# RWKV-7 recurrence on one core: odd units in the opposite partition halves, one PSUM bank per unit, and y as r·P times the state plus one product with [u; v]

## The chip, the cores and the metric

One core of one Trainium2 chip. The metric is the device time of one execution in microseconds. Three runs of the kernel before gave 2138.86, 2139.52 and 2139.69 us; the median is 2139.52. An effect of about 0.2%, some 4.3 us, can be told from no change.

## The reference

One inference step of a decoder trunk with two layers, for a prompt group (16 meta tokens and 256 prompt tokens, 272 in all) and a sample group of 8 sequences with one token each. Layer A is RWKV-7 time mixing with 64 heads of 64 channels, layer B sliding-window attention. All numbers are float32. What the change touches is layer A's recurrence over the 272 prompt tokens:

```python
def rwkv7_step(S, inp):
    r, d, k, v, kk, b = inp
    sa = jnp.einsum('bhij,bhj->bhi', S, kk)
    S = S * d[:, :, None, :] - sa[..., None] * b[:, :, None, :] + v[..., None] * k[:, :, None, :]
    return S, jnp.einsum('bhij,bhj->bhi', S, r)
...
S_fin, y = lax.scan(rwkv7_step, S0.astype(f32),
                    (tm(r_h), tm(d_h), tm(k_h), tm(v_h), tm(kk), tm(b_h)))
```

The result y is then normalised per head, gated and projected; the final state S is an output.

## The kernel before

**Chunks.** The scan runs in five chunks per head: four of 64 tokens and one of 16. P is the running product of the decays inside a chunk. With v the values of a chunk, and u the corrections that the term sa·b makes, a chunk is
- W = (kk·P)ᵀ times the state + a masked score matrix times v,
- u = TT·W, where TT solves the triangular system of the chunk,
- state = (state + BKᵀ[u; v]) times the decay,
- y = (r·P)ᵀ times the state at the start + masked scores times u and v.

**Units, groups and halves.** A unit u is two channel planes of 128 (index j), each with two heads in its two partition halves (q = 0, 1); H(q) is half q. Sixteen units; a group o is two units, an even and an odd one, 8 heads. For each head, X[c] holds 128 rows: H(q) first the state and later u, the other half v. So one product over 128 rows takes the state's and v's part together.

**What is prepared.** `prep_e` (L945) writes KB (keys and b over P) and E, two tiles of 128x2x544: for each chunk 64 columns of kk·P, then 64 of r·P. E1 is a copy of E0's upper half (L968). `scores` (L971) multiplies KB with E into two PSUM banks of [128, 512], one for each q. From each bank ACT copies the triangular parts into F and ND (L1005, L1006) for the solve, and DVE writes the masked scores: for v into the other half of E (L1007), for u into a tile RB (L1009). Even units, and some of the steps of the odd ones, use the two buffers of the pool `pe`; odd units alternate them with the single-bank pools `pc` and `py`. `substitute` (L1040) and `solve` (L1076) make TT for a group.

**The chain** (L1144). For each chunk, with three blocks on PE and pauses between them:
- S1: W into a bank of `pc` (L1173, 8 products), and y's part of state and v into a bank of `py` (L1177, 8 products). ACT copies W to SBUF (L1180, L1183).
- S2: TT times W, again into the bank of W (L1188, 8 products of 64 rows, or of 16 in the last chunk). ACT copies u over the state in X (L1190).
- S3: the state's growth (L1191, 8 products over 128 rows) and y's part of u (L1193, 8 products over 64 rows), both into the bank of `py`. DVE adds the growth to the state and applies the decay (L1201, L1202, L1204), ACT and DVE copy the state to the next X (L1207), ACT copies y to Y (L1209).

In both units a head with q = 0 takes W, u and y in partitions 0 to 63 and one with q = 1 in 64 to 127. In the first chunk the state is zero, and POOL clears that half of X[0] (L1140).

After the chain, `group_norm` (L1229) normalises Y on DVE and turns it back: for j = 0 to 3 three transposes into one bank, of `py` for even j and `pc` for odd j (L1246), which DVE reads (L1247).

**What sets the order.** PE's order is written out: `drive` (L599) puts out pieces of the projection products, each 6 products of L208 to L210 with 280 columns, and between two pieces lets the streams (`preps`, `main` with chain, scores and solve, `group_norm`, `decodes`) put out their next block when they have paused for the number of pieces that they yielded. The chain yields 5 pieces ahead of S1, 2 ahead of S2, 3 ahead of S3; group_norm 36 ahead of its first transposes and 3 ahead of each further one. Each engine works through its own queue in order. The other engines' orders come from the framework's scheduler, which also places the semaphores: for PSUM it keeps readers and writers of one tile apart, readers on different engines too.

Of the kernel before, what the change touches and what calls it, by code (L numbers as in the profile page):

```python
# [22 lines left out]
E = 4096  # L23
# [86 lines left out]
class Kernel:  # L110
# [10 lines left out]
    def run(self):  # L121
        nc, tc = self.nc, self.tc
        with contextlib.ExitStack() as st:
            pool = lambda n, bufs=1, **k: st.enter_context(tc.tile_pool(name=n, bufs=bufs, **k))
            self.cp = pool("const")
            self.wp = pool("wts", 5)
            self.pm = pool("pm", 3, space=PSUM)
            self.pp = pool("pp", 1, space=PSUM)
            self.pe = pool("pe", 2, space=PSUM)
            self.pc = pool("pc", 1, space=PSUM)  # L130
            self.py = pool("py", 1, space=PSUM)
# [11 lines left out]
            self.phase_a()  # L143
            self.close("mix")
# [11 lines left out]
            self.close("gB", "g1", "st1", "wx1", "g0", "at", "res")  # L156
# [788 lines left out]
    def prep_e(self, u):  # L945

        nc, rp = self.nc, self.rp
        V, A, G = nc.vector, nc.scalar, nc.gpsimd
        tt = V.tensor_tensor
        MU = ALU.mult  # L950
        kT, rT, kk, a, cl = (self.U[u][n] for n in ('kT', 'rT', 'kk', 'a', 'cl'))
        Pp = self.Pp
        ch = lambda x: x[:, :, :256].rearrange("p q (c t) -> p q c t", t=64)
        pch = Pp[:, :, :260].rearrange("p q (c t) -> p q c t", t=65)
        KB = self.KB
        tt(KB[:, :, 0:4, 64:128], ch(kT), ch(cl), op=MU)
# [6 lines left out]
        ech = lambda e: e[:, :, :512].rearrange("p q (c t) -> p q c t", t=128)  # L963
        tt(ech(E[0])[:, :, :, 0:64], ch(kk), pch[:, :, :, 0:64], op=MU)
        tt(ech(E[0])[:, :, :, 64:128], ch(rT), pch[:, :, :, 1:65], op=MU)
        tt(E[0][:, :, 512:528], kk[:, :, 256:272], Pp[:, :, 260:276], op=MU)
        tt(E[0][:, :, 528:544], rT[:, :, 256:272], Pp[:, :, 261:277], op=MU)
        A.copy(E[1][64:128], E[0][64:128])  # L968
        self.U[u]['E'] = E

    def scores(self, u):  # L971
# [5 lines left out]
        banks = lambda nm: [self.bank(p, f"ps_{nm[0]}{q}{nm[1]}") for q, p in  # L977
                            enumerate((self.pc, self.py) if next(turn) else (self.pe, self.pe))]
# [6 lines left out]
        RB = rp.tile([128, 2, L], F32, tag="RB", bufs=3, name=f"RB{u}")  # L985
        BK = rp.tile([128, 2, 5, 128], F32, tag="BK", bufs=3, name=f"BK{u}")
        self.U[u].update(RB=RB, BK=BK)
        inst = lambda a, r, cs: a[r, i0:i0 + 8].rearrange("p (a c) t -> p a c t", c=4)[:, :, cs]
        bc = lambda m, *s: m.unsqueeze(1).unsqueeze(1).to_broadcast(s)
        for c0 in (0, 2):  # L990
# [4 lines left out]
            with self.pe_order():  # L995
                for j in range(2):
                    for c in range(2):
                        for q in (1, 0):
                            o = 128 * (c0 + c)
                            nc.tensor.matmul(ps[q][:, j, c], KB[H(q), j, c0 + c, 64 * q:64 * q + 128],  # L1000
                                             E[q][H(q), j, o:o + 128], start=True, stop=True)
            for q in range(2):
                pv, kr, br = ps[q], H(1 - q), H(q)
                r1, r2 = slice(64 * q, 64 * q + 32), slice(64 * q + 32, 64 * q + 64)
                A.copy(inst(self.F, r1, cs), pv[r1, :, :, 0:64])  # L1005
                A.copy(inst(self.ND, r2, cs), pv[r2, :, :, 32:64])  # L1006
                tt(E[q][kr, :, 128 * c0:128 * c0 + 256].rearrange("p a (c t) -> p a c t", c=2), pv[kr],  # L1007
                   bc(self.cst(C_MASK, 128, kr), 64, 2, 2, 128), op=MU)
                tt(RB[br, :, 64 * c0:64 * c0 + 128].rearrange("p a (c t) -> p a c t", c=2), pv[br, :, :, 64:128],  # L1009
                   bc(self.cst(C_MASK + 64, 64, br), 64, 2, 2, 64), op=MU)  # L1010
        yield next(gap)
        ps = [b[:, :64].rearrange("p (a h t) -> p a h t", a=2, h=2) for b in banks(("sc", f"4_{u}"))]
        with self.pe_order():
            for j in range(2):
                for q in (1, 0):
                    nc.tensor.matmul(ps[q][:, j], KB[H(q), j, 4, 64 * q:64 * q + 128], E[q][H(q), j, 512:544],
                                     start=True, stop=True)
        for q in range(2):
            pv, kr, br = ps[q], H(1 - q), H(q)
            r1 = slice(64 * q, 64 * q + 32)  # L1020
            m = self.cst(C_MASK, 128, kr).rearrange("p (h t) -> p h t", h=2)[:, :, 0:16]
            A.copy(self.ND[r1, 16 + i0 // 4:18 + i0 // 4, 0:16], pv[r1, :, 0])
            tt(E[q][kr, :, 512:544].rearrange("p a (h t) -> p a h t", h=2), pv[kr],
               m.unsqueeze(1).to_broadcast((64, 2, 2, 16)), op=MU)
            tt(RB[br, :, 256:272], pv[br, :, 1],
               self.cst(C_MASK + 64, 16, br).unsqueeze(1).to_broadcast((64, 2, 16)), op=MU)
# [99 lines left out]
    def load_x(self, o):  # L1126
# [12 lines left out]
        for q in range(2):  # L1139
            G.memset(X[0][H(q), q], 0.0)  # L1140
# [3 lines left out]
    def chain(self, o):  # L1144
# [11 lines left out]
        heads = [(j, q) for j in range(4) for q in range(2)]  # L1156
        E = lambda j, q: us[j // 2]['E'][q][:, j % 2]
        S = FS
        decay = lambda c: PC[:, :, c:c + 1].to_broadcast((128, 4, 64))
        for c in range(5):  # L1160
# [4 lines left out]
            R = lambda q: slice(64 * q, 64 * q + n)  # L1165

            ry = lambda q: H(q) if c < 4 else slice(64 * q + 32, 64 * q + 48)
            yield (5 if c else 3), (None if c or not o else self.after(2, ('g', o - 1)))
            wu = self.bank(self.pc, f"ps_wu{o}_{c}").rearrange("p (k a i) -> p k a i", k=2, a=4)
            sy = self.bank(self.py, f"ps_sy{o}_{c}").rearrange("p (k a i) -> p k a i", k=2, a=4)  # L1170
            with self.pe_order():
                for j, q in heads:
                    mm(wu[R(q), 0, j], E(j, q)[:, 128 * c:128 * c + n], x[:, q, j], start=True, stop=True)  # L1173

                for j, q in heads:
                    out, k = (H(q), 128 * c + 64) if c < 4 else (slice(64 * q, 64 * q + 48), 496)
                    mm(sy[out, 1, j], E(j, q)[:, k:k + out.stop - out.start], x[:, q, j], start=j == 0, stop=False)  # L1177
            W = rp.tile([128, 4, 64], F32, tag="W", name=f"W{o}_{c}")
            if c < 4:
                A.copy(W, wu[:, 0])  # L1180
            else:
                for q in range(2):
                    A.copy(W[R(q)], wu[R(q), 0])  # L1183
            yield 2
            with self.pe_order():
                for j, q in heads:
                    lhs = TT[H(q), 4 * j + c] if c < 4 else TT[R(q), 16 + j, 0:16]
                    mm(wu[R(q), 1, j], lhs, W[R(q), j], start=True, stop=True)  # L1188
            for q in range(2):
                A.copy(x[R(q), q], wu[R(q), 1])  # L1190
            grow = lambda j, q, stop: mm(sy[H(q), 0, j], us[j // 2]['BK'][:, j % 2, c, H(q)], x[:, q, j],  # L1191
                                         start=False, stop=stop)
            of_u = lambda j, q, stop: mm(sy[ry(q), 1, j], us[j // 2]['RB'][R(q), j % 2, 64 * c:64 * c + n],  # L1193
                                         x[R(q), q, j], start=False, stop=stop)
            yield 3
            with self.pe_order():
                for i, f in enumerate((grow, of_u) if c < 4 else (of_u, grow)):
                    for j, q in heads:
                        f(j, q, i == 1 and j == 3)
            if c:  # L1200
                V.tensor_tensor(S, S, sy[:, 0], op=AD)  # L1201
                V.tensor_tensor(S, S, decay(c), op=MU)  # L1202
            else:
                V.tensor_tensor(S, sy[:, 0], decay(c), op=MU)  # L1204
# [3 lines left out]
            for q in range(2):  # L1208
                A.copy(self.Y[64 * (c % 2):64 * (c % 2) + n, c // 2, :, q], sy[ry(q), 1])  # L1209
# [3 lines left out]
        dma(self.O['wkv'][o], FS)  # L1213

# [14 lines left out]
    def group_norm(self, o):  # L1229
# [10 lines left out]
        for j in range(4):  # L1240
# [3 lines left out]
            ps = self.bank((self.py, self.pc)[j % 2], f"ps_yt{o}_{j}")  # L1244
# [699 lines left out]
```

## Time and profile before

| what | value |
|---|---|
| median of three runs | 2139.52 us (2138.86 to 2139.69) |
| span of the profiled execution | 2135.9 us; what lies around it is 3.6 us against that median |
| PE / DVE / ACT / POOL busy, share of the span | 98% / 80% / 59% / 6% |
| TensorE clock granted | 0.97 to 1.00 in every stretch |
| recurrence (first S1 to last S3) | 276.6 to 1252 us of the span |

The profile is of one execution. Its timeline gives, per row, the start in us, the length, engine, line, operation, output and inputs, shape and count; where an engine was idle ahead of it, the idle time and what ended it follow in brackets. Its view by groups gives busy us (the union of the instructions), the mean length of one in ns, and the idle time of the engine just before them. A float32 product leaves two records on PE. Names are those of the program, with buffer numbers left out.

### The profile page before, as it was taken

To read this page: it belongs to the slowest core of one execution; us is meant where nothing else is said; L and a number is where in the kernel's file an instruction comes from. 1 tells how busy PE (TensorE), PEld (TensorE's weight loads), DVE (VectorE), ACT (ScalarE), POOL (GpSimd) and SP (SyncE) were. 2 spreads that over 40 slices of the span, in tenths; PEclk is the share of its full clock that TensorE was granted. 3 is DMA by queue.
4 is the path that set the end of the run, shared out by engine and by line. 5 is a ranking of instruction groups with operands and counts; after the bars stand their busy time and mean duration, and the time that the engine had idled before them with its cause. 6 is when DMAs were issued, how large, how long until landed. Compare 5 with 4: busy or idle time off the path is not lost.

```text
span 2135.9 us, 56097 instructions
## 1 busy us (share of the span) xinstructions
PE 2093.4 (98%) x21548; PEld 1989.4 (93%) x21548; DVE 1706.2 (80%) x4080; ACT 1261.2 (59%) x2757; POOL 136.5 (6%) x196
## 2 busy tenths in 40 slices
PE   9999999999999999999999999999999999999997
PEld 7999998899899989999989999999999999999997
DVE  7867767787687777888978787987888888878885
ACT  3457756576765667766675445565565555644443
POOL 0011100001010010100200000100000000000000
PEclk9999999999999999999999999999999999999999
DMA  7998667658756766777656777757445454567774
GB/s 257 316 318 248 192 203 229 210 178 278 220 169 193 252 228 184 219 226 207 203 152 219 219 230 247 244 184 228 144 147 167 140 157 134 179 205 248 224 224 134
DMA packets 276357, 446.30 MB, mean 209 GB/s; under 512 B 54056, under 2 KB 97768, under 8 KB 275696
## 3 DMA queue, kind: packets, MB, share of 16 engines
q1 hardware_dynamic: 275656, 441.66, 66.7%
q8 instruction: 169, 2.77, 0.5%
q10 hardware_dynamic: 432, 1.05, 0.1%
q14 instruction: 100, 0.82, 0.1%
HBM read 381.69 MB, written 65.03 MB: 209 GB/s over the span
## 4 chain that ended last, share of the span: by engine, by line
PE 89%; DVE 4%; DMA 3%; ACT 2%; issue 1%; SPq 1%; POOL 0%; DVEq 0%; POOLq 0%; ACTq 0%
PE ps_z L208 6%; PE ps_z L209 6%; PE ps_z L210 5%; PE ps_v L208 3%; PE ps_r L208 3%; PE ps_ob L208 3%; PE ps_ob L210 3%; PE ps_ob L209 3%; PE ps_k L208 3%; PE ps_v L209 3%; PE ps_v L210 3%; PE ps_r L209 3%; PE ps_r L210 3%; PE ps_q L208 3%; PE ps_q L210 3%; PE ps_q L209 3%
## 5 line engine op out<-in xcount | busy, mean ns | idle before, releaser
L208 PE MATMUL ps_z<-mhlm,whi_z 128*128 128x280 f32 x512 | 158.7, 310 | 0.4 <-ACT st L779 0.4
L208 PE MATMUL ps_q<-bmh,whi_qb 128*128 128x264 f32 x512 | 149.9, 293 | 0.1
L209 PE MATMUL ps_z<-mhlm,whi_z 128*128 128x280 f32 x512 | 149.9, 293 | 0.0
L210 PE MATMUL ps_z<-mhlm,wlo_z 128*128 128x280 f32 x512 | 149.5, 292 | 0.0
L208 PE MATMUL ps_z<-bmh,whi_zb 128*128 128x264 f32 x512 | 147.4, 288 | 0.0
L210 PE MATMUL ps_q<-bmh,wlo_qb 128*128 128x264 f32 x512 | 145.7, 284 | 0.6 <-DVE wlo_qb L187 0.6
L209 PE MATMUL ps_q<-bml,whi_qb 128*128 128x264 f32 x512 | 145.6, 284 | 0.0
L209 PE MATMUL ps_z<-bml,whi_zb 128*128 128x264 f32 x512 | 145.5, 284 | 0.0
L210 PE MATMUL ps_z<-bmh,wlo_zb 128*128 128x264 f32 x512 | 145.4, 284 | 0.0
L208 PE MATMUL ps_ob<-ghi,whi_ob 128*128 128x264 f32 x512 | 145.3, 285 | 0.0
L209 PE MATMUL ps_ob<-glo,whi_ob 128*128 128x264 f32 x512 | 144.6, 283 | 0.0
L210 PE MATMUL ps_ob<-ghi,wlo_ob 128*128 128x264 f32 x512 | 144.6, 284 | 0.0
L185 ACT CAST whi_ob<-raw_ob 128x512 fp32r<-128x512 f32 x128 | 79.1, 621 | 96.9 <-PE ps_ob L209 76.5
L185 ACT CAST whi_oa<-raw_oa 128x512 fp32r<-128x512 f32 x128 | 79.4, 621 | 90.7 <-PE ps_oa L209 32.4
L187 DVE TENSOR_TENSOR wlo_r<-raw_r,whi_r 128x512 fp32r<-128x512 f32 x128 | 87.7, 689 | 49.2 <-ACT whi_r L185 46.3
L208 PE MATMUL ps_v<-mhlm,whi_v 128*128 128x280 f32 x384 | 121.5, 316 | 1.2 <-ACT st L779 1.2
L208 PE MATMUL ps_k<-mhlm,whi_k 128*128 128x280 f32 x384 | 119.2, 310 | 0.9 <-ACT st L779 0.9
L187 DVE TENSOR_TENSOR wlo_v<-raw_v,whi_v 128x512 fp32r<-128x512 f32 x128 | 87.2, 686 | 39.5 <-ACT whi_v L185 38.8
L185 ACT CAST whi_v<-raw_v 128x512 fp32r<-128x512 f32 x128 | 79.0, 618 | 65.3 <-PE ps_v L209 39.5
L185 ACT CAST whi_zb<-raw_zb 128x512 fp32r<-128x512 f32 x128 | 78.2, 619 | 62.6 <-PE ps_z L209 40.0
L187 DVE TENSOR_TENSOR wlo_oa<-raw_oa,whi_oa 128x512 fp32r<-128x512 f32 x128 | 87.5, 689 | 32.8 <-ACT whi_oa L185 31.2
L209 PE MATMUL ps_v<-mhlm,whi_v 128*128 128x280 f32 x384 | 112.7, 293 | 0.0
(474 smaller groups left out, 7681.5 us busy)
## 6 DMA issues: line engine op xcount, KB each, us to landing
raw_k<-a_w_rkvz SPq DMA_DIRECT2D x128, 256.0 KB
raw_v<-a_w_rkvz SPq DMA_DIRECT2D x128, 256.0 KB
raw_r<-a_w_rkvz SPq DMA_DIRECT2D x128, 256.0 KB
raw_z<-a_w_rkvz SPq DMA_DIRECT2D x128, 256.0 KB
raw_oa<-a_w_out SPq DMA_DIRECT2D x128, 256.0 KB
raw_qb<-b_w_qz SPq DMA_DIRECT2D x128, 256.0 KB
raw_zb<-b_w_qz SPq DMA_DIRECT2D x128, 256.0 KB
raw_ob<-b_w_o SPq DMA_DIRECT2D x128, 256.0 KB
```

The lines of the kernel that those rows point to most:

```text
L185: self.nc.scalar.copy(hi, src)
L187: return self.nc.vector.tensor_tensor(lo, src, hi.bitcast(F32), op=ALU.subtract)
L208: mm(ps, wh, xh, start=start, stop=False)
L209: mm(ps, wh, xl, start=False, stop=False)
L210: return mm(ps, wl, xh, start=False, stop=stop)
```

## The change

The mirrored layout. In odd units the products of a head with half q now land in half 1-q of PSUM where W, TT and y are concerned, while X, KB, E and the state stay as they were. The rows of F and ND that the odd units write are exchanged to match (`r ^ 64 * odd`), and Y is read back through an access pattern of its own (`turned_y`).

The banks. During phase A the pools `pc` and `py` are closed, and one pool `pcy` with a single tile of two banks takes their place: bank f belongs to unit f of the group and holds all four regions of a chunk (W, u, growth, y). The odd units' scores, their transposes and group_norm's transposes take the same tile, bank by bank.

The terms of y. E is now [128, 5, 2, 272]: E[:,0] and E[:,1] are kk·P and the masked scores of v for the two halves, E[:,2] is r·P, and E[:,3] and E[:,4] hold the masked scores of y for all 128 rows, u's and v's. RB is gone. y is (r·P)ᵀ times the state (64 rows, in S2 behind TT, not in the first chunk) plus one product over 128 rows with [u; v] (in S3). In the first chunk W is a product over the 64 rows of v alone, so X[0] is not cleared. In the last chunk POOL clears W, and TT and the product run over all 64 rows.

```diff
@@ run
+            self.close("py", "pc")
+            self.pcy = self.open("pcy", 1, space=PSUM)
             self.phase_a()
+            self.close("pcy")
+            self.single_banks()
...
+    def two_banks(self, name):
+
+        return self.pcy.tile([128, 2, 512], F32, tag="b", name=name)
@@ prep_e
-        E = [rp.tile([128, 2, 544], F32, tag=f"E{q}", bufs=3, name=f"E{q}_{u}") for q in range(2)]
...
-        A.copy(E[1][64:128], E[0][64:128])
+        E = rp.tile([128, 5, 2, L], F32, tag="E", bufs=3, name=f"E_{u}")
+        tt(ch(E[:, 0]), ch(kk), pch[:, :, :, 0:64], op=MU)
+        tt(ch(E[:, 2]), ch(rT), pch[:, :, :, 1:65], op=MU)
...
+        A.copy(E[64:128, 1], E[64:128, 0])
@@ scores
+        rows = lambda q, j, a, b: E[H(q), q:3:2 - q, j, a:b]
...
-                A.copy(inst(self.F, r1, cs), pv[r1, :, :, 0:64])
-                A.copy(inst(self.ND, r2, cs), pv[r2, :, :, 32:64])
-                tt(E[q][kr, :, 128 * c0:128 * c0 + 256].rearrange("p a (c t) -> p a c t", c=2), pv[kr],
-                   bc(self.cst(C_MASK, 128, kr), 64, 2, 2, 128), op=MU)
-                tt(RB[br, :, 64 * c0:64 * c0 + 128].rearrange("p a (c t) -> p a c t", c=2), pv[br, :, :, 64:128],
-                   bc(self.cst(C_MASK + 64, 64, br), 64, 2, 2, 64), op=MU)
+                for r, a, t0 in ((64 * q, self.F, 0), (64 * q + 32, self.ND, 32)):
+                    A.copy(inst(a, slice(r ^ 64 * odd, (r ^ 64 * odd) + 32), cs), pv[r:r + 32, :, :, t0:64])
+                tt(out(q, kr), pv[kr, :, :, 0:64], bc(self.cst(C_MASK, 64, kr), 64, 2, 2, 64), op=MU)
+                tt(out(3 + q, slice(0, 128)), pv[:, :, :, 64:128], bc(self.cst(C_MASK + 64, 64), 128, 2, 2, 64), op=MU)
@@ load_x
-        for q in range(2):
-            G.memset(X[0][H(q), q], 0.0)
@@ chain
-        heads = [(j, q) for j in range(4) for q in range(2)]
+        heads = [(f, k, q) for k in range(2) for f in range(2) for q in range(2)]
...
-            wu = self.bank(self.pc, f"ps_wu{o}_{c}").rearrange("p (k a i) -> p k a i", k=2, a=4)
-            sy = self.bank(self.py, f"ps_sy{o}_{c}").rearrange("p (k a i) -> p k a i", k=2, a=4)
+            two = self.two_banks(f"ps_ch{o}_{c}")
+            ps = two.rearrange("p f (r k i) -> p f r k i", r=4, k=2)
...
-                for j, q in heads:
-                    mm(wu[R(q), 0, j], E(j, q)[:, 128 * c:128 * c + n], x[:, q, j], start=True, stop=True)
-
-                for j, q in heads:
-                    out, k = (H(q), 128 * c + 64) if c < 4 else (slice(64 * q, 64 * q + 48), 496)
-                    mm(sy[out, 1, j], E(j, q)[:, k:k + out.stop - out.start], x[:, q, j], start=j == 0, stop=False)
+                for f, k, q in heads:
+                    v = H(1 - q) if c == 0 else slice(0, 128)
+                    mm(ps[R(q ^ f), f, 0, k], E(f, q, v, k, 64 * c, 64 * c + n), x[v, q, 2 * f + k],
+                       start=True, stop=True)
...
+                G.memset(W, 0.0)
                 for q in range(2):
-                    A.copy(W[R(q)], wu[R(q), 0])
+                    A.copy(W2[R(q)], part(0, R(q)))
...
+                for f, k, q in heads:
+                    h, j = q ^ f, 2 * f + k
+                    mm(ps[H(q), f, 1, k], TT[H(h), 4 * j + c if c < 4 else 16 + j], W[H(h), j], start=True, stop=True)
+
+                for f, k, q in heads if c else ():
+                    mm(ps[ry(q ^ f), f, 3, k], E(f, 2, H(q), k, *ty), x[H(q), q, 2 * f + k], start=k == 0, stop=k == 1)
...
+                for f, k, q in heads:
+                    add(ps[H(q), f, 2, k], us[f]['BK'][:, k, c, H(q)], x[:, q, 2 * f + k])
+
+                for f, k, q in heads:
+                    add(ps[ry(q ^ f), f, 3, k], E(f, 3 + q, slice(0, 128), k, *ty), x[:, q, 2 * f + k])
@@ group_norm
-            ps = self.bank((self.py, self.pc)[j % 2], f"ps_yt{o}_{j}")
+            if j % 2 == 0:
+                two = self.two_banks(f"ps_yt{o}_{j}")
+            ps = two[:, j % 2]
```

How the instructions stand now, at three places. First PE, the blocks S2 and S3 of chunk 2 in group 3 (units 6 and 7; the pieces of projection products between them are left out). Before:

```order
L1188 MATMUL ps_wu3_2_10843<-W3_2_10864,TT3_9598 64x64 [waits Activation_49]
L1188 MATMUL ps_wu3_2_10843<-W3_2_10864,TT3_9598 64x64 x7
...
L1191 MATMUL ps_sy3_2_10844<-X0_3_9320,BK6_8280 64x64 [waits Activation_49] x2
L1191 MATMUL ps_sy3_2_10844<-X0_3_9320,BK6_8280 64x64 x2
L1191 MATMUL ps_sy3_2_10844<-X0_3_9320,BK7_9299 64x64 x4
L1193 MATMUL ps_sy3_2_10844<-X0_3_9320,RB6_8279 64x64 x4
L1193 MATMUL ps_sy3_2_10844<-X0_3_9320,RB7_9298 64x64 x4
```

And of the change:

```order
L1201 MATMUL ps_ch3_2_10762<-W3_2_10774,TT3_9532 64x64 [waits Activation_49]
L1201 MATMUL ps_ch3_2_10762<-W3_2_10774,TT3_9532 64x64 x7
L1204 MATMUL ps_ch3_2_10762<-X0_3_9257,E_6_8080 64x64 x2
L1204 MATMUL ps_ch3_2_10762<-X0_3_9257,E_7_9230 64x64 x2
L1204 MATMUL ps_ch3_2_10762<-X0_3_9257,E_6_8080 64x64 x2
L1204 MATMUL ps_ch3_2_10762<-X0_3_9257,E_7_9230 64x64 x2
...
L1210 MATMUL ps_ch3_2_10762<-X0_3_9257,BK7_9236 64x64 x2
L1213 MATMUL ps_ch3_2_10762<-X0_3_9257,E_6_8080 64x64 x2
L1213 MATMUL ps_ch3_2_10762<-X0_3_9257,E_7_9230 64x64 x2
L1213 MATMUL ps_ch3_2_10762<-X0_3_9257,E_6_8080 64x64 x2
L1213 MATMUL ps_ch3_2_10762<-X0_3_9257,E_7_9230 64x64 x2
```

The units alternate after every two products. Eight products of y with the state have moved from S1 to the end of S2, and the second half of S3 reads E in place of RB. Second, PE at group_norm's transposes in group 0, without the products between them. Before:

```order
L1246 MATMUL ps_yt0_0_5388<-consts_78,Y_1737 128x128 x3
...
L1246 MATMUL ps_yt0_1_5423<-consts_78,Y_1737 128x128 x3
...
L1246 MATMUL ps_yt0_2_5480<-consts_78,Y_1737 128x128 [waits DVE_49]
L1246 MATMUL ps_yt0_2_5480<-consts_78,Y_1737 128x128 x2
...
L1246 MATMUL ps_yt0_3_5595<-consts_78,Y_1737 128x128 [waits DVE_49]
L1246 MATMUL ps_yt0_3_5595<-consts_78,Y_1737 128x128 x2
```

And of the change:

```order
L1271 MATMUL ps_yt0_0_5365<-consts_78,Y_1742 128x128 x3
...
L1271 MATMUL ps_yt0_0_5365<-consts_78,Y_1742 128x128 [waits DVE_49]
L1271 MATMUL ps_yt0_0_5365<-consts_78,Y_1742 128x128 x2
...
L1271 MATMUL ps_yt0_2_5456<-consts_78,Y_1742 128x128 [waits DVE_49]
L1271 MATMUL ps_yt0_2_5456<-consts_78,Y_1742 128x128 x2
...
L1271 MATMUL ps_yt0_2_5456<-consts_78,Y_1742 128x128 [waits DVE_49]
L1271 MATMUL ps_yt0_2_5456<-consts_78,Y_1742 128x128 x2
```

Before, j = 2 waits for DVE's read of j = 0 and j = 3 for that of j = 1; now j = 1, 2 and 3 each wait for the read of the one just before. Third, ACT at the scores of unit 11 (chunks 2 and 3, copies into F). Before:

```order
L1005 COPY F_1733<-ps_sc12_11_13869 32x2x128 [waits PE_49]
L1006 COPY F_1733<-ps_sc12_11_13869 32x2x2x32
L1005 COPY F_1733<-ps_sc02_11_13868 32x2x128 [waits PE_49]
L1006 COPY F_1733<-ps_sc02_11_13868 32x2x2x32
L185 CAST whi_z_0_14_14026<-raw_z_0_14_14024 128x512 [waits DMAHW7_49,DVE_49,PE_49]
```

And of the change:

```order
L1019 COPY F_1738<-ps_sc2_11_13759 32x2x128 [waits PE_49]
L1019 COPY F_1738<-ps_sc2_11_13759 32x2x2x32
L195 CAST whi_z_0_14_13916<-raw_z_0_14_13914 128x512 [waits DMAHW4_49,DVE_49,PE_49]
...
L1019 COPY F_1738<-ps_sc2_11_13759 32x2x128 [waits DVE_49]
L1019 COPY F_1738<-ps_sc2_11_13759 32x2x2x32
```

The second bank's copies have moved behind DVE's masks of the first bank, and behind the cast that stood after them.

More of the change, by code (lines that the diff above doesn't have):

```diff
@@ L155, in run, with single_banks @@
             self.wx = None
[L156 removed]
+            self.close("gB", "g1", "st1", "wx1", "g0", "at", "res", "py", "pc")
+    def single_banks(self):
+        self.pc, self.py = (self.open(n, 1, space=PSUM) for n in ("pc", "py"))
+    def two_banks(self, name):
+        return self.pcy.tile([128, 2, 512], F32, tag="b", name=name)
     def open(self, name, bufs=1, **k):
@@ L976, in scores, with banks @@
         turn = iter((0, odd, 0, odd, 0))
-        banks = lambda nm: [self.bank(p, f"ps_{nm[0]}{q}{nm[1]}") for q, p in
-                            enumerate((self.pc, self.py) if next(turn) else (self.pe, self.pe))]
+        def banks(nm):
+            if next(turn):
+                two = self.two_banks(f"ps_{nm[0]}{nm[1]}")
+                return [two[:, q] for q in range(2)]
+            return [self.bank(self.pe, f"ps_{nm[0]}{q}{nm[1]}") for q in range(2)]
         V, A, G = nc.vector, nc.scalar, nc.gpsimd
@@ L1207, in chain @@
                     (V.tensor_copy if q else A.copy)(X[c + 1][H(q), q], S[H(q)])
-            for q in range(2):
-                A.copy(self.Y[64 * (c % 2):64 * (c % 2) + n, c // 2, :, q], sy[ry(q), 1])
+            for h in range(2):
+                A.copy(self.turned_y(c, h, n), part(3, slice(ry(h).stop - n, ry(h).stop)).rearrange("p f (k i) -> p f k i", k=2))
             if c % 2 or c == 4:
@@ L1213, in chain, with turned_y @@
         dma(self.O['wkv'][o], FS)
+    def turned_y(self, c, h, n):
+        y = self.Y[64 * (c % 2):64 * (c % 2) + n, c // 2]
+        (step, rows), free = y.ap[0], y.ap[1:]
+        assert [list(a) for a in free] == [[128, 4], [64, 2], [1, 64]], free
+        return type(y)(y.tensor, y.offset + 64 * h, [[step, rows], [320 - 128 * h, 2], [128, 2], [1, 64]])
     def variance(self, o, c):
```

68 lines of the change are left out of this document (29 added, 39 removed).

## The prediction

> **What bounds the kernel now.** I read the stretch of the recurrence first: busy time of each engine between 276 and 1256 us (the columns after the length are PE, PE's weight loads, DVE, ACT, POOL, each with its instructions, then the granted clock, the DMA share and GB/s).
>
> ```profile
> core 0 of [0], span 2135.9 us
> core 0: us, PE busy (x) PEld busy (x) DVE busy (x) ACT busy (x) POOL busy (x), PEclk, DMA share, GB/s
> 276.00:1256.00 980.00, 961.27 (x12209) 895.92 (x12208) 778.33 (x1722) 637.49 (x1404) 78.58 (x115) 0.99 0.68 208
> ```
>
> PE is busy 98% of these 980 us at a clock of 0.99, DVE 79%, ACT 65%, and the DMA engines are at 0.68. So the stretch is bound by PE, and what shortens PE's own list shortens the kernel one for one, as long as nobody new makes PE wait. Who makes it wait today, in us, times and the longest:
>
> ```profile
> PE ps_so L1089 <- DVE TN L1068: 5.0, 2, 2.8
> PE ps_yt L1246 <- DVE vT L1247: 4.0, 1, 4.0
> ```
>
> These two are the longest waits of the whole execution. They are small, but both are places that the change touches.
>
> **The price of a block on PE.** The recurrence is cut into small blocks that stand between the large projection products (L208 to L210). A busy PE says little about such a block, because instructions overlap; so I take the timeline of PE and measure from the last projection product ahead of a block to the second one behind it, less two regular steps. First product of a chunk (S1, ps_wu and ps_sy):
>
> ```profile
> 289.51 0.29 PE L209 MATMUL ps_k<-mhlm,whi_k 128*128 128x280 f32 x1
> 289.64 0.29 PE L210 MATMUL ps_k<-mhlm,wlo_k 128*128 128x280 f32 x1
> 289.86 0.69 PE L1173 MATMUL ps_wu<-X,E 128*64 128x64 f32 x16
> 290.38 0.64 PE L1177 MATMUL ps_sy<-X,E 128*64 128x64 f32 x16
> 290.94 0.40 PE L208 MATMUL ps_k<-mhlm,whi_k 128*128 128x280 f32 x1
> 291.18 0.29 PE L209 MATMUL ps_k<-mhlm,whi_k 128*128 128x280 f32 x1
> ```
>
> A regular step is 289.64 - 289.51 = 0.13. S1 costs 291.18 - 289.64 - 0.26 = 1.28 us for 32 records (each f32 product leaves two). The product with TT (S2) and the last block of a chunk (S3):
>
> ```profile
> 293.76 0.29 PE L210 MATMUL ps_k<-mhlm,wlo_k 128*128 128x280 f32 x1
> 293.98 0.68 PE L1188 MATMUL ps_wu<-W,TT 64*64 64x64 f32 x16
> 294.59 0.40 PE L208 MATMUL ps_k<-mhlm,whi_k 128*128 128x280 f32 x1
> 294.82 0.29 PE L209 MATMUL ps_k<-mhlm,whi_k 128*128 128x280 f32 x1
> ```
>
> ```profile
> 297.68 0.29 PE L210 MATMUL ps_k<-mhlm,wlo_k 128*128 128x280 f32 x1
> 297.90 0.69 PE L1191 MATMUL ps_sy<-X,BK 128*64 128x64 f32 x16
> 298.51 0.68 PE L1193 MATMUL ps_sy<-X,RB 64*64 64x64 f32 x16
> 299.13 0.40 PE L208 MATMUL ps_k<-mhlm,whi_k 128*128 128x280 f32 x1
> 299.36 0.29 PE L209 MATMUL ps_k<-mhlm,whi_k 128*128 128x280 f32 x1
> ```
>
> S2 costs 0.80 us for 16 records. S1 and S2 together give a fixed price of 0.32 and 0.030 per record. S3 costs 1.42 with 32 records, 0.14 more than S1: in its middle PE goes from tiles of 128 rows to tiles of 64 (0.61 from L1191 to L1193, where L1173 to L1177 took 0.52).
>
> **How many tiles run at once** is the open number. Today the products alternate between two tiles, and 0.030 per record means that two overlap (alone, one would take 0.059). The changed S2 names four tiles of 64x64 in turn: rows and columns (0,0), (64,64), (64,0), (0,64). The nearest rows are those of the block solve, where L1089 uses four 32x32 tiles and L1107 two (here: busy us, mean ns | idle before):
>
> ```profile
> L1173 PE MATMUL ps_wu<-X,E 128*64 128x64 f32 x512 | 22.3, 228 | 2.3 <-DVE X L1207 1.4 <-ACT X L1207 0.9
> L1188 PE MATMUL ps_wu<-W,TT 64*64 64x64 f32 x512 | 21.8, 224 | 0.0
> L1177 PE MATMUL ps_sy<-X,E 128*64 128x64 f32 x512 | 20.5, 222 | 0.0
> L1089 PE MATMUL ps_so<-TN,Noff 32*32 32x16 f32 x1024 | 10.3, 184 | 5.0 <-DVE TN L1068 5.0
> L1107 PE MATMUL ps_so<-TN,F 32*32 32x32 f32 x512 | 9.6, 192 | 0.9 <-DVE TN L1102 0.9
> ```
>
> Four tiles made 1024 records in 10.3 us, two made 512 in 9.6: double the rate. Those four share neither rows nor columns; the new four do. But L1173's two tiles share all 128 rows and L1188's share none, and 512 records take 22.3 and 21.8 us, so shared rows cost nothing visible. The bounds are 0.059 (one at a time) and 0.010 (L1089's rate); I take 0.015, four at a time, being the rate of two, doubled as in the solve.
>
> The Trainium skill speaks against it: "TensorE: Matmul & The Clock Gate", Part 3 (packing small matmuls), says that a weight load runs beside a matmul only where the row groups differ. By that rule the pairs with equal rows would not overlap and S2 would keep two at a time, which is the first rival below; L1173 against L1188 disagrees with the rule for tiles of 128 rows, and no row shows it for four tiles of 64.
>
> **The sum on PE** (8 groups of 5 chunks: 32 chunks after the first, 8 first ones):
> - S1 in 32 chunks: 16 records instead of 32, 1.28 to 0.80: -15.4.
> - First chunks, without a state: S1 becomes 16 records on four tiles, 0.32 + 16 x 0.015 = 0.56 (-0.72); S2 with TT alone 0.80 to 0.56 (-0.24): 8 x 0.96 = -7.7.
> - S2 in 32 chunks: 32 records, 0.32 + 32 x 0.015 = 0.80: 0.
> - S3 in 40 chunks: no change of tile, 1.42 to 1.28: -5.6.
>
> Together -28.7.
>
> **What DVE, ACT and POOL gain** is credited with nothing, because PE does not wait for it:
>
> ```profile
> L1007 DVE TENSOR_TENSOR E<-ps_sc,consts 64x512 f32<-64x512 f32 x64 | 43.6, 682 | 10.0 <-ACT F L1006 9.7
> L1009 DVE TENSOR_TENSOR RB<-ps_sc,consts 64x256 f32<-64x256 f32 x64 | 27.0, 422 | 0.9
> L968 ACT COPY E<-E 64x1088 f32<-64x1088 f32 x16 | 17.6, 1100 | 2.0 <-DVE E L967 1.4
> ```
>
> The masks become two of 256 elements: 64 x (682 - 422) = 16.6 us less on DVE. The copy of E halves: some 8 us less on ACT. The memset of W (POOL) may start when S2 of chunk 3 is done, and is needed some eight pieces of the products later.
>
> **The waits it adds.** All readers and writers of the new two-bank tile are ordered as of one tile. In group_norm the transposes of j=1, 2, 3 now each wait for DVE's read of the one before (today j waits for j-2). What stands behind them is everything on PE. First and last of the 8 groups, PE and DVE:
>
> ```profile
> 377.21 0.49 PE L1246 MATMUL ps_yt<-consts,Y 128*128 128x128 f32 x3
> 383.99 0.90 PE L1246 MATMUL ps_yt<-consts,Y 128*128 128x128 f32 x3 [3.97 <-DVE vT L1247]
> ```
>
> ```profile
> 383.46 0.47 DVE L1247 SCALAR_TENSOR_TENSOR vT<-ps_yt,par,vT 128x272 f32<-128x272 f32 x1
> ```
>
> ```profile
> 1272.88 0.49 PE L1246 MATMUL ps_yt<-consts,Y 128*128 128x128 f32 x3
> 1275.54 0.49 PE L1246 MATMUL ps_yt<-consts,Y 128*128 128x128 f32 x3
> ```
>
> ```profile
> 1273.30 0.50 DVE L1247 SCALAR_TENSOR_TENSOR vT<-ps_yt,par,vT 128x272 f32<-128x272 f32 x1
> ...
> 1278.16 0.50 DVE L1247 SCALAR_TENSOR_TENSOR vT<-ps_yt,par,vT 128x272 f32<-128x272 f32 x1
> ```
>
> Group 0: the read of j=0 ends at 383.93, j=1 stood at 377.21, so PE waits 6.7 where it waited 4.0: +2.7. Group 7: j=2 waits 0.9, and j=3, then at 1276.4, for 1278.66: +3.1 in all. The same reading gives 0, 0, 0, 1.3, 0.3 and 1.9 for groups 1 to 6. Together +9.3; 0 if DVE gets there earlier, and I keep 9.
>
> In odd scores ACT's copies of the second bank now wait for DVE's masks of the first; substitute and then the solve (the 5.0 above) stand behind them. The worst of the two solves that wait today:
>
> ```profile
> 887.53 0.26 ACT L1006 COPY F<-ps_sc 32x128 f32<-32x128 f32 x1
> ```
>
> ```profile
> 890.28 0.43 DVE L1009 TENSOR_TENSOR RB<-ps_sc,consts 64x256 f32<-64x256 f32 x1
> ```
>
> The copies would end 890.71 + 0.62 - 887.79 = 3.5 later. The bounds are 0 and 7 for both; I take 1, since the masks in between are four times 0.26 shorter.
>
> U's copies now wait for the y product behind TT in the same block, 0.24 to 0.48 later. The tightest place:
>
> ```profile
> 333.28 0.75 ACT L1190 COPY X<-ps_wu 16x256 f32<-16x256 f32 x2
> ```
>
> ```profile
> 334.11 0.62 PE L1193 MATMUL ps_sy<-X,RB 16*16 16x64 f32 x16
> ```
>
> 0.08 is left there, at one of 40 chunks (1.1 us of ACT just ahead of it is the copy of E that halves): nothing. The next S1 waits for Y's copies at its start instead of 0.52 into it; L1177's idle time of 0.0 says that they are long done: nothing.
>
> **Sum:** -28.7 + 9.3 + 1 = -18.4, from a span of 2135.9 to 2117.5. The median of the three runs, 2139.52, lies 3.6 above this span; the forecast is 2121.
>
> **The rivals.**
> - Two tiles at a time (0.030): S2 in 32 chunks pays +15.4, first chunks gain only 3.8: -15.4 - 3.8 + 15.4 - 5.6 = -9.4, and the waits eat it: 2140. For it: no row shows four tiles that share rows and columns. Against: L1173 beside L1188. 0.20.
> - PE held at the two-bank tile, the slower side: group_norm's three waits in 8 groups cost as much as in group 0 today or more. At 6.7 each they are 54, giving 2139.5 - 28.7 + 54 = 2165; it decides from 3.6 per group. For it: DVE is at 79% here, and PE comes to it sooner. Against: three groups of eight show no wait at all. 0.08.
> - One tile at a time (0.059), if sharing rows or columns serializes: S2 of 32 records 2.21, 32 x 1.41 = +45, first chunks +4, S1 -15.4, S3 -5.6, waits +10: 2178. 0.04.
> - DVE, at 79%, keeps PE from using half of the gain elsewhere: -14 + 10 and less wait, about 2132. 0.04.
>
> **How the numbers follow.** The forecast has 0.64, with a range of its own from 2110 (hardly any wait) to 2129. Taking in the two-tile rival with its spread of 3, 2108 to 2143 leaves out the slower tails and a little below. About 0.2% (4.3 us) is what a measurement of this kernel can tell from no change. Faster by more: 0.64 + 0.04 and 0.03 of the two-tile case, 0.71; within: 0.14; slower: 0.08 + 0.04 + 0.03, 0.15.
>
> **What would show it.** S2 of 32 records at 0.8 between projection products means four tiles, 1.28 two, over 2 one. S1 must be 0.8, S3 1.28. Waits of ps_yt on DVE over 9 us, and of ps_so over 6, would show the holds. I am wrong if S2 shows 1.28, or if the waits of ps_yt pass 20 us.

## The result and the profile after

The changed kernel takes 2123.87 us (median of 5 runs, 2121.02 to 2132.89) against 2139.52 before (2138.75 to 2144.49): a ratio of 0.9938, with an interval from 0.992 to 0.9956. Two later series on other occasions gave 2123.81 and 2125.62 (ratios 0.9935 and 0.9927), so the gain is 14 to 16 us. The execution profiled first is the slowest of its five (2132.89, span 2131.1); a second profile of the same kernel (the run `e0_again`, span 2124.3) is used where totals are compared.

The timeline of PE around one chunk of group 0, after (start, us, engine, line, operation, tile, shape, count). First S1:

```profile
294.22 0.29 PE L220 MATMUL ps_k<-mhlm,wlo_k 128*128 128x280 f32 x1
294.44 0.69 PE L1187 MATMUL ps_ch<-X,E 128*64 128x64 f32 x16
295.06 0.40 PE L218 MATMUL ps_k<-mhlm,whi_k 128*128 128x280 f32 x1
295.29 0.29 PE L219 MATMUL ps_k<-mhlm,whi_k 128*128 128x280 f32 x1
```

Then S2 and S3:

```profile
297.87 0.29 PE L220 MATMUL ps_k<-mhlm,wlo_k 128*128 128x280 f32 x1
298.09 0.46 PE L1201 MATMUL ps_ch<-W,TT 64*64 64x64 f32 x16
298.37 0.41 PE L1204 MATMUL ps_ch<-X,E 64*64 64x64 f32 x16
...
298.95 0.29 PE L219 MATMUL ps_k<-mhlm,whi_k 128*128 128x280 f32 x1
```

```profile
301.81 0.29 PE L220 MATMUL ps_k<-mhlm,wlo_k 128*128 128x280 f32 x1
302.02 0.69 PE L1210 MATMUL ps_ch<-X,BK 128*64 128x64 f32 x16
302.54 0.64 PE L1213 MATMUL ps_ch<-X,E 128*64 128x64 f32 x16
...
303.34 0.29 PE L219 MATMUL ps_k<-mhlm,whi_k 128*128 128x280 f32 x1
```

By the measure of the prediction S1 is 295.29 - 294.22 - 0.26 = 0.81, S2 of 32 records 0.82, S3 1.27. S2 has twice the records of before at the price of before: L1201's 16 records take 0.28 until L1204 starts, where L1173's 16 took 0.52 on two tiles. Over all chunks the medians are 0.81, 0.82 and 1.27, and 0.59 for the first chunk's S1 and S2. The starts of the single records, which the rows above merge, show why: in S2 four records start within 0.02 us, one on each of the four tiles, and past the first four a new four comes every 0.058 us; in S1 and S3, with two tiles, two start together, again every 0.058 us.

The stretch of the recurrence, 980 us from the first chunk on as before (columns as there), first profile:

```profile
282.00:1262.00 980.00, 948.38 (x12156) 885.21 (x12155) 768.31 (x1754) 634.92 (x1411) 68.31 (x109) 0.99 0.68 210
```

PE is still the bound, but idle for 980 - 948.4 = 31.6 us where it was 18.7: the blocks are cheaper and the waits have grown. The waits of PE in the second profile of the changed kernel (us, times, longest):

```profile
PE ps_yt L1271 <- DVE vT L1272: 9.4, 4, 7.7
PE ps_so L1098 <- DVE TN L1077: 5.3, 2, 4.0
...
PE ps_ch L1201 <- ACT W L1192: 1.6, 2, 1.3
```

The wait of ps_yt has grown from 4.0 to 9.4 (11.0 in the first profile), and most of it stands in group 0 (7.7 and 7.3). PE and DVE there, first profile:

```profile
376.45 0.49 PE L1271 MATMUL ps_yt<-consts,Y 128*128 128x128 f32 x3
386.56 0.90 PE L1271 MATMUL ps_yt<-consts,Y 128*128 128x128 f32 x3 [7.30 <-DVE vT L1272]
```

```profile
380.35 0.93 DVE L897 SCALAR_TENSOR_TENSOR kk<-kT,par,kk 128x280 f32<-128x280 f32 x2 [4.76 <-DMA kk<-kr]
...
386.05 0.46 DVE L1272 SCALAR_TENSOR_TENSOR vT<-ps_yt,par,vT 128x272 f32<-128x272 f32 x1
```

The read that PE waits for is late because DVE had stood 4.76 us behind a transfer (3.45 before the change) and did its transposes for the solve, at 384.50, ahead of the read. The masks on DVE, now L1020 and L1021, cost what was worked out (busy us, mean ns):

```profile
L1020 DVE TENSOR_TENSOR E<-ps_sc,consts 64x256 f32<-64x256 f32 x64 | 26.8, 419 | 14.5 <-ACT F L1019 13.5
L1021 DVE TENSOR_TENSOR E<-ps_sc,consts 128x256 f32<-128x256 f32 x64 | 26.6, 415 | 0.4
```

53.4 us where it was 70.6: 17 us less on DVE.

### The profile page after: what moved, and what is told of

Its sections match the earlier page's. It is cut to its first block, busy times and chain, and to the rows that moved or that the text cites. A ratio compares the mean times of both kernels' runs of the same rounds, so it can differ in the third digit from the quotient of the medians.

```text
span 2131.1 us, 55813 instructions
## 1 busy us (share of the span) xinstructions
PE 2073.1 (97%) x21420; PEld 1971.4 (93%) x21420; DVE 1685.4 (79%) x4080; ACT 1252.9 (59%) x2757; POOL 121.5 (6%) x188
## 3 DMA queue, kind: packets, MB, share of 16 engines
q10 hardware_dynamic: 432, 1.05, 0.1%
## 4 chain that ended last, share of the span: by engine, by line
PE 60%; DVE 3%; DMA 2%; issue 1%; ACT 1%; POOL 0%; POOLq 0%; DVEq 0%; SPq 0%; ACTq 0%
PE ps_z L218 6%; PE ps_z L219 5%; PE ps_z L220 5%; PE ps_ob L218 3%; PE ps_ob L220 3%; PE ps_ob L219 3%; PE ps_q L218 3%; PE ps_q L220 3%; PE ps_q L219 3%; PE ps_oa L219 2%; PE ps_oa L218 2%; PE ps_oa L220 2%; PE ps_o L218 1%; PE ps_o L219 1%; PE ps_o L220 1%
## 5 line engine op out<-in xcount | busy, mean ns | idle before, releaser
L218 PE MATMUL ps_v<-mhlm,whi_v 128*128 128x280 f32 x384 | 121.4, 316 | 0.4 <-ACT st L789 0.4
L218 PE MATMUL ps_k<-mhlm,whi_k 128*128 128x280 f32 x384 | 120.4, 313 | 1.1 <-ACT st L789 1.1
L220 PE MATMUL ps_k<-mhlm,wlo_k 128*128 128x280 f32 x384 | 112.9, 294 | 1.2 <-issue 1.1
L219 PE MATMUL ps_k<-mhlm,whi_k 128*128 128x280 f32 x384 | 113.0, 294 | 0.0
```

Of the source, the lines that this page charges most:

```text
L218: mm(ps, wh, xh, start=start, stop=False)
L219: mm(ps, wh, xl, start=False, stop=False)
L220: return mm(ps, wl, xh, start=False, stop=stop)
```

## The experiments

All run on the chip beside the kernel before; a time is a median, a ratio is to the kernel before with its interval. First the changed kernel itself.

> The changed kernel once more, unaltered. Theory (the 9 us by which its profiled execution, 2132.9, lies above the median of its runs, 2123.9, belong to that one execution): the median is 2123 to 2125 again, and a second profile shows PE idle for some 49 us instead of 58, with the first chunk's S1 near 277 us instead of 282.3. Rival (the kernel loses them whenever it is profiled first, or by a wait of its own): idle 58 us and S1 at 282 again.

2123.81 us, 0.9935 (0.9924 to 0.9947). PE idle is 2124.3 - 2070.5 = 53.8 us, between the two expectations, and the first S1 stands at 281.2, against 282.3 in the first profile and 276.6 before the change. So the later start belongs mostly to the kernel; most of the 9 us by which the first profiled execution lay above its median belongs to that one execution.

**The order of the tiles.**

```diff
-        heads = [(f, k, q) for k in range(2) for f in range(2) for q in range(2)]
+        heads = [(f, k, q) for f in range(2) for k in range(2) for q in range(2)]
```

> The changed kernel with the products of each block ordered unit by unit, so that in S2 and in the first chunk's S1 only two tiles of 64x64 alternate at a time (four over the block). Theory (the order in which tiles are named sets how many overlap): S2 of 32 records goes from 0.82 to 1.28 us, the first chunk's S1 and S2 of 16 records from 0.59 to 0.80: 32 x 0.46 + 16 x 0.21 = +18, about 2142. Rival (PE looks far enough ahead, or a record's price is set by its size): 0.82 stays, 2124. S1 of the other chunks, 0.81, and S3, 1.28, stay by both.

2123.41 us, 0.9929 (0.9917 to 0.9941): no change. S2 in PE's timeline:

```profile
294.54 0.29 PE L220 MATMUL ps_k<-mhlm,wlo_k 128*128 128x280 f32 x1
294.75 0.47 PE L1201 MATMUL ps_ch<-W,TT 64*64 64x64 f32 x16
295.04 0.46 PE L1204 MATMUL ps_ch<-X,E 64*64 64x64 f32 x16
...
295.66 0.29 PE L219 MATMUL ps_k<-mhlm,whi_k 128*128 128x280 f32 x1
```

0.86 here, 0.87 in the median, where 1.28 was expected. That theory fell: the four tiles need not be named in turn.

**The halves.** `q ^ f` becomes `q` throughout the chain, the copies of the scores keep their rows, and y is read without the turn. One of these lines:

```diff
-                    h, j = q ^ f, 2 * f + k
+                    h, j = q, 2 * f + k
```

> The changed kernel with the odd units in the same halves as the even ones; one bank per unit and y as r.P times state plus one product with [u; v] stay. Only two tiles of 64x64 are left in S2. Theory (mirroring the halves is what lets four tiles run): S2 1.28, first chunk's blocks 0.80, about 2142, so that the new form of y alone is worth no more than the measurement can tell from the kernel before (2139.5). Rival (the bank of its own for each unit is what makes S2 fast): S2 0.82, 2124.

2138.10 us, 1.0002 (0.9993 to 1.0011). S2:

```profile
298.82 0.29 PE L220 MATMUL ps_k<-mhlm,wlo_k 128*128 128x280 f32 x1
299.03 0.68 PE L1201 MATMUL ps_ch<-W,TT 64*64 64x64 f32 x16
299.55 0.63 PE L1204 MATMUL ps_ch<-X,E 64*64 64x64 f32 x16
...
300.35 0.29 PE L219 MATMUL ps_k<-mhlm,whi_k 128*128 128x280 f32 x1
```

1.27 for the same 32 records, in the median too, and 0.81 for the first chunk's blocks. The whole gain rests on the mirrored halves; the new form of y with a bank for each unit brings nothing alone, since PE's idle time is 51.7 us here, 9.2 more than before, and that takes back what S1, S3 and the first chunks save. Whether the mirrored halves would gain as much without a bank for each unit was not tried.

**Runs on one tile.** The same line with `for q in range(2) for f in range(2) for k in range(2)`.

> The changed kernel with the products of each block ordered by q outermost, so that runs of 8 records (S1, S3) or 4 (S2) on one tile follow each other. Theory A, formed after the order by units cost only 0.05 us in S2 (a block costs 0.35 + 0.058 per record on its busiest tile, since PE runs ahead on the other tiles): no change, S1 0.81, S2 0.82 to 0.9, S3 1.28, 2124 to 2127. Rival B (records of different tiles overlap only when they stand close together): toward one record at a time, S1 up to 1.28, S3 up to 2.2, S2 up to 2.2, and a time up to 32 x 0.47 + 40 x 0.92 + 32 x 1.38 = 96 later, 2220. In between, the blocks tell how far PE runs ahead.

2139.78 us, 0.9993 (0.9977 to 1.001): between A and B. S1 is 0.87 (its runs on one tile are 4, 8 and 4 records, not two of 8 as the expectation has it), S2 with runs of 4 is 0.91, but S3, which opens with two runs of 8, 1.61:

```profile
304.30 0.29 PE L220 MATMUL ps_k<-mhlm,wlo_k 128*128 128x280 f32 x1
304.52 0.79 PE L1210 MATMUL ps_ch<-X,BK 128*64 128x64 f32 x13
305.09 0.27 PE L1213 MATMUL ps_ch<-X,E 128*64 128x64 f32 x1
305.14 0.22 PE L1210 MATMUL ps_ch<-X,BK 128*64 128x64 f32 x1
...
306.17 0.29 PE L219 MATMUL ps_k<-mhlm,whi_k 128*128 128x280 f32 x1
```

A record of L1213 starts ahead of L1210's last three, though all of L1210 stands ahead of it in the program; it is so in all 40 chunks. So PE runs ahead past a busy tile, and the statement ahead of the prediction that each engine works through its queue in order doesn't hold for PE's products on different tiles. But it doesn't run so far ahead that the order is free: the blocks explain 40 x 0.34 + 32 x 0.09 + 32 x 0.06 = 18 us. Measured are 16 by the times and 12 by the ratios; the two differ because the kernel before took 2141.35 in the series of this run and the next three, and 2137.78 in that of the changed kernel.

**Uneven tiles.**

```diff
-                    mm(ps[ry(q ^ f), f, 3, k], E(f, 2, H(q), k, *ty), x[H(q), q, 2 * f + k], start=k == 0, stop=k == 1)
+                    mm(ps[ry(q), 0, 3, k], E(0, 2, H(q), k, *ty), x[H(q), q, k], start=k + f == 0, stop=k + f == 2)
```

> The changed kernel with all products of r.P and the state on the two tiles (0,0) and (64,64), the even units' twice and the odd units' not at all (y of the odd units lacks that part). S2 keeps 32 records on four tiles, but 12, 12, 4 and 4 instead of 8 each. Theory A (0.35 + 0.058 per record on the busiest tile): 0.35 + 12 x 0.058 = 1.05, 32 x 0.23 = +7, about 2131. Rival C (a rate set by how many tiles the block names, 0.015 a record): 0.82, 2124. Rival D (two at a time as soon as the halves are not balanced): 1.28, 2139.

2129.27 us, 0.9951 (0.9931 to 0.997): 5 more than the changed kernel by the times, 3 by the ratios, where A has 7. The block is the sharper measure:

```profile
294.94 0.29 PE L220 MATMUL ps_k<-mhlm,wlo_k 128*128 128x280 f32 x1
295.15 0.46 PE L1201 MATMUL ps_ch<-W,TT 64*64 64x64 f32 x16
295.44 0.63 PE L1204 MATMUL ps_ch<-X,E 64*64 64x64 f32 x16
...
296.24 0.29 PE L219 MATMUL ps_k<-mhlm,whi_k 128*128 128x280 f32 x1
```

296.24 - 294.94 - 0.26 = 1.04, where A gave 1.05, C 0.82 and D 1.28. A holds: the tile with the most records sets the price. Each half of the rows and of the columns still has 16 records, as with 8 on each tile, so it is the tile that counts.

**The fixed part.** The products of r.P and the state go into a block of their own, a piece ahead of TT's (in this order y comes out wrong, so the run tells of times alone).

```diff
-            yield 2
+            yield 1
+            with self.pe_order():
+                for f, k, q in heads if c else ():
+                    mm(ps[ry(q ^ f), f, 3, k], E(f, 2, H(q), k, *ty), x[H(q), q, 2 * f + k], start=k == 0, stop=k == 1)
+            yield 1
             with self.pe_order():
...
-                for f, k, q in heads if c else ():
-                    mm(ps[ry(q ^ f), f, 3, k], E(f, 2, H(q), k, *ty), x[H(q), q, 2 * f + k], start=k == 0, stop=k == 1)
```

> The changed kernel with the product of r.P and the state as a block of its own, one piece of the projections after S1 and one ahead of the product with TT (which stays 2 pieces behind S1). Theory (each block costs about 0.35 us whatever is in it, between projection products): S2 of 0.82 becomes two blocks of 0.59, 32 x 0.36 = +11.5, about 2135. Rival (the fixed part is an artefact of the fit, and 16 records cost half of 32): 0.82 in all, 2124.

2140.04 us, 0.9993 (0.998 to 1.0006): 16 more than the changed kernel by the times, 12 by the ratios, where 11.5 were expected. Each half is 0.59 (here 305.87 - 305.02 - 0.26), so the fixed part holds. Between the profiles PE is busy 2081.9 - 2070.5 = 11.4 us longer, and idle 6.5 longer by a wait that the edit brought:

```profile
305.02 0.29 PE L220 MATMUL ps_k<-mhlm,wlo_k 128*128 128x280 f32 x1
305.24 0.46 PE L1200 MATMUL ps_ch<-X,E 64*64 64x64 f32 x16
...
305.87 0.29 PE L219 MATMUL ps_k<-mhlm,whi_k 128*128 128x280 f32 x1
```

```profile
PE ps_ch L1200 <- ACT W L1192: 6.3, 8, 1.6
```

The new block stands one piece behind S1 and waits, 8 times, for the copy of W from the same two-bank tile, though it doesn't read W.

**The change of the tile's rows.** The last products of y run over 64 rows, and half of the sum with [u; v] is left out.

```diff
-                    add(ps[ry(q ^ f), f, 3, k], E(f, 3 + q, slice(0, 128), k, *ty), x[:, q, 2 * f + k])
+                    add(ps[ry(q ^ f), f, 3, k], E(f, 3 + q, H(q ^ f), k, *ty), x[H(q ^ f), q, 2 * f + k])
```

> The changed kernel with the last products of y on 64 rows instead of 128, on the two tiles (0,0) and (64,64) like the kernel before (half of the sum of r.B u and r.K v is left out of y). The records of S3 stay 32 on two tiles. Theory (0.14 us of S3 before was the change of the tile's rows in the middle of a block): S3 goes from 1.28 back to 1.42, 40 x 0.14 = +5.6, about 2129. Rival (S3 became cheaper through the banks or the order, not through the rows): 1.28 stays, 2124.

2128.05 us, 0.9945 (0.9924 to 0.9965): 4 more than the changed kernel by the times, 2 by the ratios, too little for a verdict between 0 and 5.6. The block decides it:

```profile
298.52 0.29 PE L220 MATMUL ps_k<-mhlm,wlo_k 128*128 128x280 f32 x1
298.74 0.69 PE L1210 MATMUL ps_ch<-X,BK 128*64 128x64 f32 x16
299.36 0.68 PE L1213 MATMUL ps_ch<-X,E 64*64 64x64 f32 x16
...
300.20 0.29 PE L219 MATMUL ps_k<-mhlm,whi_k 128*128 128x280 f32 x1
```

300.20 - 298.52 - 0.26 = 1.42, the price of before: 0.14 is the change from 128 rows to 64 within a block.

**The waits of group_norm**, taken out of the changed kernel (six transposes at one place) and, further below, put into the kernel before (all transposes in one bank).

```diff
-            yield 3 if j else 36 if o < NU // 2 - 1 else 19
             if j % 2 == 0:
+                yield 9 if j else 36 if o < NU // 2 - 1 else 19
                 two = self.two_banks(f"ps_yt{o}_{j}")
+                for i in range(2):
+                    for c in range(3):
+                        nc.tensor.transpose(two[:, i, 128 * c:128 * c + 128],
+                                            Y[:, c, j + i].rearrange("p q i -> p (q i)"), self.ident)
             ps = two[:, j % 2]
-            for c in range(3):
-                nc.tensor.transpose(ps[:, 128 * c:128 * c + 128], Y[:, c, j].rearrange("p q i -> p (q i)"), self.ident)
```

> The changed kernel with group_norm's transposes in pairs: j=0 and 1 into the two banks at one place, then both reads, nine pieces on j=2 and 3 at one place. The end of group_norm stays in place. Theory (the waits of ps_yt on DVE cost PE one for one and come from the two banks being ordered as one tile): they fall from 11.0 to 2 or 3 us (group 0 keeps some, since DVE itself stands behind a transfer there), and the time by 8 to 9, to about 2115. Rival (PE's wait only moves to the next place that needs DVE): ps_yt falls, others rise, 2124.

2120.47 us, 0.9914 (0.9899 to 0.993), with no wait of ps_yt left; beside 0.9935 (0.9924 to 0.9947) the gain stayed open. So both kernels ran again in one series:

> The changed kernel unaltered, as the measure for the two below in the same series of runs: 2124 again, PE's waits of ps_yt between 9 and 11 us.

> The transposes in pairs once more, beside the changed kernel, since the first series left the gain open between 0 and 8 us (medians 2120.5 and 2123.8). Theory (PE's wait is worth its length): 8 less than the changed kernel. Theory formed since (in group 0 DVE itself stands 4 to 5 us behind a transfer, so of PE's 8 us there some 4 come back at the next products that need DVE, as ps_v and ps_so showed): 4 to 5 less. Rival: 0.

2125.62 us for the changed kernel (0.9927, 0.9909 to 0.9946) and 2115.75 with the pairs (0.989, 0.9876 to 0.9904): 3 less in the first series, where the two intervals overlap, and 10 less in the second, where they don't. That the pairs gain is shown; whether the 8 or the 4 to 5 is right is not. PE's idle time, 48.6 in both profiles with the pairs, is 5.2 below the changed kernel's 53.8 in the first series and 6.7 below its 55.3 in the second. The profile of the second:

```profile
PE ps_so L1098 <- DVE TN L1077: 6.6, 2, 3.8
...
PE ps_v L220 <- DVE wlo_v L197: 3.3, 2, 2.3
```

The wait of 10.6 is gone, and ps_v, which needs DVE a little later, has a new one of 3.3: part of it does come back.

```diff
-            ps = self.bank((self.py, self.pc)[j % 2], f"ps_yt{o}_{j}")
+            ps = self.bank(self.py, f"ps_yt{o}_{j}")
```

> The kernel before with all four transposes of group_norm in one bank, so that each waits for DVE's read of the one ahead, as in the changed kernel; nothing else of the change. This is the price of that wait alone. PE's waits of ps_yt go from 4.0 to about 11. Theory (worth its length): 7 more than before. Theory formed since (half comes back in group 0): 3 to 4 more. Rival (DVE catches up, nothing is lost): 0.

2141.80 us, 1.0014 (1.0004 to 1.0023): 3 more (1 to 5). PE's waits:

```profile
PE ps_yt L1246 <- DVE vT L1247: 10.1, 5, 6.2
PE ps_so L1089 <- DVE TN L1068: 3.3, 2, 2.0
```

6.1 more at ps_yt, 1.7 less at ps_so. The wait alone costs about half of its length by the medians, and not all of it: the full 7 lie outside the interval.

**A version that beats both.** The pairs, and the solve's first products later:

```diff
-        yield 24 if o < 5 else 27
+        yield 30 if o in (0, 5) else 24 if o < 5 else 27
```

> The transposes in pairs, and the first products of the solve six pieces later for groups 0 and 5, the two in which PE waited for DVE's transposes (4.0 and 1.2). Theory: ps_so falls from 5.3 to under 1 and the time by 4 to 5 against the pairs alone. Rival (the first chain starts later and the wait moves to its first products): no change against the pairs alone.

2108.72 us, 0.9855 (0.984 to 0.9871): 7 less than the pairs, 17 less than the changed kernel. The wait of ps_so on DVE, 6.6 with the pairs, falls to one:

```profile
PE ps_so L1098 <- DVE TN L1077: 0.4, 1, 0.4
```

That is more than the 4 to 5 expected, and the windows of four microseconds show what else went. The changed kernel, first profile, at the solve of group 0 (the third column from the right is the granted clock):

```profile
252.00:256.00 4.00, 2.64 (x21) 2.41 (x19) 3.81 (x14) 3.27 (x8) 0.00 (x0) 1.00 0.83 271
256.00:260.00 4.00, 1.11 (x83) 1.11 (x87) 3.43 (x7) 2.29 (x7) 0.86 (x2) 0.73 0.76 274
260.00:264.00 4.00, 4.00 (x74) 3.96 (x67) 1.11 (x2) 3.05 (x5) 0.00 (x0) 0.50 0.14 24
```

The kernel before:

```profile
256.00:260.00 4.00, 4.00 (x22) 4.00 (x21) 0.86 (x2) 4.00 (x11) 0.20 (x1) 0.61 0.52 170
```

And the best version there:

```profile
256.00:260.00 4.00, 4.00 (x150) 3.81 (x149) 1.65 (x4) 4.00 (x9) 0.00 (x0) 1.00 1.00 368
260.00:264.00 4.00, 2.92 (x112) 2.65 (x110) 2.76 (x6) 3.69 (x7) 0.20 (x1) 1.00 0.88 278
```

In the changed kernel PE waits 4.3 us and then works at half its clock; in the best version its products of the solve (128 records from 257.46) neither wait nor run slower.

## Why the prediction was right

2121 was forecast and 2123.87 measured, by the mechanism that was forecast: cheaper blocks on PE, less what the new waits take back.

**S2 on four tiles: right, for half of its reason.** The prediction took 0.015 per record because four tiles at once should have twice the rate of two. The price was right (0.82 for 0.80), and the bounds held. But it is no rate per record: 0.35 + 0.058 per record on the busiest tile gives 1.28 (16 on one tile), 0.82 (8), 0.58 (4) and 1.05 (12), and the runs with two tiles (1.27) and with 12 records on one (1.04) bear it out; the run in another order is near it (0.87 for 0.82). Where the records are even the two ways of counting give the same price, which is why the prediction came out. The two-tile rival is the run with the same halves, and it came out at 2138 where 2140 was worked out.

**The Trainium skill's rule against it.** S2's pairs with equal rows do overlap: 0.82 with four tiles against 1.27 with two. The Trainium skill, "TensorE: Matmul & The Clock Gate", Part 3, has the weight load overlap only where row groups differ; the measured price for tiles of 64x64 doesn't fit that, and the measurement decides. The same part of the Trainium skill tells of a reorder window for weight loads. The run in another order (0.87) and that tile by tile (0.91) agree with a window; in S3 of the second the products themselves also start out of order.

**S1, first chunks, S3: right.** S1 32 x (1.28 - 0.81) = 15.0 for 15.4; first chunks 8 x (1.28 - 0.59 + 0.81 - 0.59) = 7.3 for 7.7, the 0.56 being 0.59; S3 40 x 0.14 = 5.6, with the run on half the rows for its reason. S2 costs 0.4. Together some 27.5 of the 28.7.

**The waits: the sum right by luck, its parts not.** Against the profile before, PE's idle time rose from 2135.9 - 2093.4 = 42.5 to 53.8, by 11.3, for 9.3 + 1. In it ps_yt has +5.4 to +7.0 for 9.3: group 0 waits 3.2 to 3.7 longer (2.7 expected), group 7 at most 1.0 (3.1 expected). ps_so has +0.3 to +0.5 for +1, but not as put: group 0's wait grew from 2.2 to about 4, that of group 5 shrank from 2.8 to 1.2. Whether ACT's copies behind the masks did that was not tried. Three waits make up for it that were not foreseen or were put at nothing (ranges of three profiles of the changed kernel): the W copy with 1.2 to 2.9 (S1 is 0.47 shorter, and S2 still stands two pieces behind it), the copy of u ahead of S3 with 0.5 to 0.9 at one chunk, and one block of the scores' products with 0.8 to 1.0 behind DVE's masks, whose cause was not followed.

**What the sum lacked** is the granted clock. The table ahead of the prediction has it at 0.97 to 1.00 in every stretch; in windows of four microseconds it falls to 0.5. Adding 4 x (1 - clock) over the windows below 0.97, without the last ones of the execution, gives 10.1 us before, 15.3 in two later profiles of the changed kernel and 18.7 in its first. In part of these windows PE stands idle anyway, so the sums are upper estimates. With them 2135.9 - 27.5 + 11.3 + 5 = 2124.7, and the second profile's span is 2124.3. At the solve of group 0 the loss is 3.4 us, before 1.7; at group 0's transposes it is 3.4 in both. The rest is scattered and not traced to the change: the run on half the rows, with the same two-bank tile, has 10.2 in its profile. So the clock is enough for the 3 us between 2121 and 2124, but that the change causes all of it is not shown. The DVE rival (2132) did not come about: DVE lost 17 us and PE kept its gain.

## What to carry to other kernels

Price a block of small products by its busiest tile: count the records on each tile, and spread them evenly; products on other tiles are free as long as no long run on one tile stands ahead of them (runs of 4 records cost 0.09 a block, two of 8 at its head 0.34). Keep one row size within a block, and put products that can share a block together, since in this kernel each block between large products costs 0.35 us by itself. Two banks ordered as one tile add waits at every use that had two buffers; move those uses into pairs, and look first at the places where the engine waited for is itself held up by a transfer.

## What was not expected of the hardware

A pause of PE is paid twice when it is long. Behind a wait of 4.3 us PE's clock was 0.50 for the four microseconds from 260 (0.73 in the window ahead). The Trainium skill, "TensorE: Matmul & The Clock Gate", Part 1, states that an idle window of about 3.4 us halves the clock until PE has been busy as long; these rows agree, though before the change a wait of 2.2 us at the same place (up to 254.09) was followed by a window at 0.61 as well. The loss comes in one size: the sums over an execution are 5.1 us in the best version, 10.2 on half the rows, 15.3 and 18.7 in the changed kernel, all near multiples of 1.7, which is 3.4 us at half the clock. With the pairs the sum was 13.6 in the first series and 10.1 in the second, so single executions of one kernel differ by such steps. And PE takes products past a busy tile from later in its list: with runs of 4 records the price rose from 0.82 to 0.91, with two runs of 8 at the head of the block from 1.27 to 1.61.
